# A 4096 x 4096 matmul with gelu: other load order for A, another plan for turning A and for the split operands, and a tail that adds in PSUM

## The chip, the cores and the metric

The kernel runs on one core of a Trainium2 chip. The metric is the device time of one execution in microseconds (us); several executions of each kernel were timed, and medians and ranges are given. Most executions lie within 0.3% of their kernel's median. So differences of a few microseconds out of 1560 need several runs, and the profile's single holes (stretches in which TensorE has no matmul to run) are read beside the times.

TensorE is called PE below, VectorE DVE, ScalarE ACT, GpSimd POOL and SyncE SP. PSUM is the buffer that the matmuls write here. The kernel gives each tile of results (128x512 in f32) a bank of it by name, and the next product writes that bank after another engine has read it out.

## The reference

```python
def setup_inputs():
    m, k, n = 4096, 4096, 4096
    return {"a": np.random.randn(m, k).astype(np.float32),
            "b": np.random.randn(k, n).astype(np.float32)}

def reference(a, b):
    x = np.matmul(a, b)
    return 0.5 * x * (1 + np.tanh(np.sqrt(2 / np.pi) * (x + 0.044715 * x**3)))
```

## The kernel before

The kernel multiplies in f16 with a seven-product scheme. A, B and the output are cut into four quadrants; `A22` is the lower right one. There are 16 **groups**: a block of 512 rows of both row halves of A against a block of 512 columns of both column halves of B. Each group computes M1 to M7, each a product of a sum of two A quadrants with a sum of two B quadrants (or one quadrant alone), from `aS` and `bS`, which DVE makes 2048 elements per partition at a time. In groups 10 to 15 the pair M3/M5, and in groups 13 to 15 also M2/M1, are cut once more by the same scheme; the B operands of that second level ("split operands") are made in earlier groups and parked in DRAM. One **step** of the schedule is 16 matmuls of 512 columns, 3.45 us.

Five parts matter here. *First*, the order in which the first row block is loaded, turned (transposed by DVE) and weighed. `A12_1` is a load of the second K chunk of A12, `T` a transpose, `W` a weighing (ACT squares the rows, to decide at the end whether f16 was safe), `S` a sum:

```python
    for n, whats in (
        (0, "A11_0 B12_0 T11_0 W11_0 B11_0 A21_0 A12_0 B22_0 B21_0"),
        (4, "T21_0 W21_0 A22_0"),
        (6, "T12_0 W12_0"),
        (8, "A11_1+B12_1+B22_1"),
        (9, "T22_0 W22_0 A12_1+B21_1a B21_1b"),
        (14, "T11_1 W11_1 B11_1a A22_1 B11_1b"),
        (16, "T12_1 W12_1:0-4"),
        (17, "W12_1:4-16 A21_1"),
        (18, "S2 S3 T22_1"),
        (23, "T21_1"),
        (34, "W22_1:0-1"),
        # ... one row of W22_1, then of W21_1, a step
```

*Second*, the plan by which later row blocks of A are loaded into one of two staging buffers, turned and weighed; a buffer comes free five steps after its transpose, when ACT has weighed it in four portions:

```python
        free_at = [0, 0]
        for (quad, h), n in zip(halves, turns(gi)):
            at_step(max(n - LOAD_AHEAD, free_at.pop(0)), load, (load_half, (mb, quad, h)))
            free_at.append(n + 5)
            at_step(n, turn_half, mb, quad, h)
            for x in range(4):
                at_step(n + 1 + x, weigh_rows, mb, quad, h, ...)     # cut
            if h and quad in ("12", "21"):
                at_step(n + 5, weigh_half, mb, int(quad[0]) - 1)
```

*Third*, where the split operands are made. An entry of `MAKES` is (group, product, quarter, column block, product it is for); it starts five sums of DVE, one a step, and each goes out to DRAM from one of three `bS` buffers:

```python
MAKES = (
    (6, 1, 0, 1, "M3"), (6, 2, 1, 1, "M5"), (6, 3, 2, 3, "M3"), (6, 4, 2, 3, "M5"),
    (7, 1, 3, 0, "M2"), (8, 2, 3, 2, "M3"), (8, 4, 0, 2, "M5"), (8, 5, 3, 2, "M1"),
    (9, 2, 0, 0, "M3"), (9, 2, 2, 0, "M5"), (9, 4, 2, 3, "M1"), (9, 5, 3, 3, "M2"),
    (10, 2, 2, 2, "M2"), (10, 4, 0, 0, "M1"),
)
```

*Fourth*, `TWO_GROUPS`, the steps at which ACT squares B for the same check. *Fifth*, the end: in the last groups M6 is added on DVE to what M3 and M2 left, and ACT takes the gelu of it:

```python
    def settle_fresh(gi, name, i, X, Y):
        # ... M3, M2, M4 cut
        elif name == "M1":
            m1, x7 = keep("m5", X, 2), post["x7", i]
            tt(x7, x7, m1, ALU.add)
        elif name == "M6":
            y = post.pop(("x1", i))
            tt(y, X, y, ALU.add)
            flush()
            waiting.append((gi, i, 1, 1, y, y))      # gelu and store later
```

## Time and profile before

| | us |
|---|---|
| median of the kernel before, 4 runs | 1572.32 (1568.32 to 1575.03) |
| span of the profiled run | 1570.0 |

The prediction below takes this span apart. I measured holes from start to start: the time between the starts of two matmuls, less the pitch of 215.8 ns (512 columns) or 109.1 ns (256 columns). That counts the half clock too, which the waits do not.

The next lines are PE's instructions in order of time, kernel before: start in us, length, engine, line of the kernel, operation, output <- inputs, shapes, how many; in brackets the idle time before it and what released it.

```profile
85.79 0.61 PE L468 MATMUL accX<-bS,aS 128*128 128x512 f16 x2 [0.55 <-DVE aS L430]
88.40 15.24 PE L468 MATMUL accX<-bS,aS 128*128 128x512 f16 x62 [2.00 <-DVE aS L430]
...
440.58 3.63 PE L468 MATMUL accX<-bR,aS 128*128 128x512 f16 x16 [1.97 <-DVE aS L430]
447.46 26.20 PE L468 MATMUL accX<-bS,aS 128*128 128x512 f16 x120 [1.52 <-ACT m L579]
...
955.48 8.77 PE L468 MATMUL accX<-bK,aS 128*128 128x512 f16 x32 [2.79 <-DVE aS L933]
```

The last row shows how a hole goes on costing: 32 matmuls need 6.9 us at 215.8 ns but took 8.77, because eight of its first eleven ran at half clock. At all of these holes but the one at 447.46 PE waits for DVE, and DVE waits for something else. The list of all waits (engine, what it makes, its line, what released it: us in total, times, longest) names what:

```profile
POOL stage L257 <- ACT stage L271: 106.4, 10, 26.9
...
DVE aT L221 <- DMA stage<-in_a_dram: 69.5, 15, 10.8
...
DVE bS L933 <- DMA k_split<-bS: 26.9, 13, 5.7
```

DVE in order of time shows the same three at the places where PE stood:

```profile
436.45 2.37 DVE L221 STREAM_TRANSPOSE aT<-stage 128x1024 uint32<-128x1024 uint32 x2 [7.23 <-DMA stage<-in_a_dram]
...
942.29 1.23 DVE L933 TENSOR_TENSOR bS<-bK 128x2048 f16<-128x2048 f16 x1 [3.73 <-DMA k_split<-bS]
...
953.06 1.23 DVE L933 TENSOR_TENSOR bS<-bK 128x2048 f16<-128x2048 f16 x1 [2.92 <-DMA k_split<-bS]
```

At 436 the transpose waits for a load that POOL issued late, since its staging buffer was held by ACT's weighing. At 942 and 953 a sum waits until an earlier sum's buffer has been written out.

### The profile page before, as it was taken

To read this page: it belongs to the slowest core of one execution; us is meant where nothing else is said; L and a number is where in the kernel's file an instruction comes from. 1 tells how busy PE (TensorE), PEld (TensorE's weight loads), DVE (VectorE), ACT (ScalarE), POOL (GpSimd) and SP (SyncE) were. 2 spreads that over 40 slices of the span, in tenths; PEclk is the share of its full clock that TensorE was granted. 3 is DMA by queue.
4 is the path that set the end of the run, shared out by engine and by line. 5 is a ranking of instruction groups with operands and counts; after the bars stand their busy time and mean duration, and the time that the engine had idled before them with its cause. 6 is when DMAs were issued, how large, how long until landed. Compare 5 with 4: busy or idle time off the path is not lost. (4 is left out here: it accounts for less than half of the span.)

```text
span 1570.0 us, 22246 instructions
## 1 busy us (share of the span) xinstructions
PE 1547.9 (99%) x8110; PEld 794.1 (51%) x8110; DVE 1139.6 (73%) x1357; ACT 600.8 (38%) x1322; POOL 462.5 (29%) x830
## 2 busy tenths in 40 slices
PE   9999999999999999999999999999999999999998
PEld 4444444444444444444444443554746457677674
DVE  1598888889778886765557647878749677776774
ACT  5446555465643642211554211121355523232232
POOL 7664433431124311122231222221333312132230
PEclk9999999999999999999999999999999999999999
DMA  9999999994789987799998989898999958688692
GB/s 176 183 224 294 269 304 273 286 216 81 188 220 298 292 299 283 278 416 328 277 283 233 411 317 345 307 414 272 279 263 315 351 156 306 237 283 308 234 332 108
DMA packets 202790, 429.41 MB, mean 274 GB/s; under 512 B 20400, under 2 KB 102320, under 8 KB 200624
## 3 DMA queue, kind: packets, MB, share of 16 engines
q0 software_dynamic: 141472, 265.34, 65.6%
q1 hardware_dynamic: 61200, 162.56, 27.1%
q8 instruction: 66, 1.08, 0.3%
q14 instruction: 52, 0.43, 0.1%
HBM read 340.79 MB, written 162.53 MB: 321 GB/s over the span
## 5 line engine op out<-in xcount | busy, mean ns | idle before, releaser
L468 PEld LDWEIGHTS <-aS 128*128 128x128 f16 x4192 | 410.2, 98 | 510.4 <-issue 7.9
L468 PE MATMUL accX<-bK,aS 128*128 128x512 f16 x1536 | 336.0, 380 | 3.3 <-DVE aS L933 3.3
L933 DVE TENSOR_TENSOR aS<-aT 128x2048 f16<-128x2048 f16 x182 | 217.1, 1219 | 94.7 <-PE accX L468 70.6
L468 PEld LDWEIGHTS <-aT 128*128 128x128 f16 x1600 | 156.6, 98 | 189.2 <-issue 1.4
L919 POOL DMA_DIRECT2D bK<-k_M x236 | 124.8, 534 | 401.5 <-PE accX L468 119.3
L257 POOL DMA_DIRECT2D bR<-in_b_dram x320 | 173.1, 543 | 210.5 <-DMA bR<-in_b_dram 98.2
L271 ACT ACTIVATE stage<-stage 128x512 f16<-128x512 f16 (+1 forms) x320 | 169.5, 532 | 141.0 <-DVE aT L221 108.8
L468 PE MATMUL accY<-bK,aS 128*128 128x512 f16 x896 | 195.0, 379 | 2.2 <-DVE aS L933 1.2
L612 ACT ACTIVATE x<-x 128x512 f32<-128x512 f32 x128 | 78.3, 628 | 251.8 <-DVE x L621 251.7
L468 PE MATMUL accX<-bS,aS 128*128 128x512 f16 x704 | 155.1, 382 | 4.1 <-DVE aS L430 2.5
L430 DVE TENSOR_TENSOR aS<-aT 128x2048 f16<-128x2048 f16 (+1 forms) x112 | 134.0, 1201 | 25.8 <-PE accX L468 14.6
L550 PEld LDWEIGHTS <-aS 128*128 128x128 f16 x1440 | 140.9, 98 | 23.1 <-issue 1.1
L430 DVE TENSOR_TENSOR bS<-bR 128x2048 f16<-128x2048 f16 x110 | 133.5, 1218 | 18.6 <-PE accX L468 13.6
L311 ACT ACTIVATE square<-bR 128x1024 bf16<-128x1024 f16 x120 | 123.1, 1048 | 42.7 <-DVE energy L621 42.0
L257 POOL DMA_DIRECT2D stage<-in_a_dram x144 | 84.5, 593 | 178.8 <-ACT stage L271 106.4
L221 DVE STREAM_TRANSPOSE aT<-stage 128x1024 uint32<-128x1024 uint32 (+1 forms) x61 | 76.0, 1278 | 80.0 <-DMA stage<-in_a_dram 69.5
L579 ACT COPY x<-accX 128x512 f32<-128x512 f32 x116 | 67.8, 586 | 173.0 <-PE accX L468 172.7
L933 DVE TENSOR_TENSOR bS<-bK 128x2048 f16<-128x2048 f16 x70 | 84.3, 1219 | 27.1 <-DMA k_split<-bS 26.9
L621 DVE TENSOR_TENSOR x<-accY,x 128x512 f32<-128x512 f32 x116 | 77.2, 688 | 30.1 <-ACT y L612 20.3
L468 PE MATMUL accY<-bK,aT 128*128 128x512 f16 x448 | 97.8, 379 | 0.0
L468 PE MATMUL accX<-bK,aT 128*128 128x512 f16 x448 | 97.8, 379 | 0.0
L579 ACT COPY m<-accX 128x512 f32<-128x512 f32 x76 | 43.2, 581 | 119.8 <-PE accX L468 95.1
(70 smaller groups left out, 1518.4 us busy)
## 6 DMA issues: line engine op xcount, KB each, us to landing
bK<-k_M POOLq DMA_DIRECT2D x272, 512.0 KB, 10.1
bK<-k_split POOLq DMA_DIRECT2D x90, 512.0 KB, 6.7
bR<-in_b_dram POOLq DMA_DIRECT2D x320, 128.0 KB, 7.4
k_M<-bS SPq DMA_DIRECT2D x80, 512.0 KB, 6.5
k_split<-bS SPq DMA_DIRECT2D x70, 512.0 KB, 7.1
out_dram<-y SPq DMA_DIRECT2D x128, 256.0 KB, 6.3
out_dram<-x SPq DMA_DIRECT2D x128, 256.0 KB, 7.3
stage<-in_a_dram POOLq DMA_DIRECT2D x112, 256.0 KB, 8.4
```

The source lines that it names most:

```text
L221: nc.vector.transpose(dst[:, :, x, :], src)
L257: nc.gpsimd.dma_start(out=dst, in_=src)
L271: nc.scalar.activation(src, src, ACT.Square, accum_out=dst)
L311: nc.scalar.activation(t[:, :], src, ACT.Square)
L430: nc.vector.tensor_tensor(out=x, in0=y, in1=z, op=ALU.add if o[2] > 0 else ALU.subtract)
L468: nc.tensor.matmul(acc[:, :], sa[:, j // 2, i * P : (i + 1) * P, j % 2], sb[:, j, :], start=start and j == 0, stop=stop and j == 3, skip_g ...
L550: nc.tensor.matmul(banks[chain, i][:, :] if wide else out, sa[:, j // 2, r * P : (r + 1) * P, j % 2], sb[:, : NC] if wide else sb[:, j * N ...
L579: nc.scalar.copy(out=t[:, :], in_=src[:, :])
L612: nc.scalar.activation(y[:, :], src[:, :], ACT.Gelu_apprx_tanh)
L621: nc.vector.tensor_tensor(out=o[:, :], in0=x[:, :], in1=y[:, :], op=op)
L919: nc.gpsimd.dma_start(out=dst, in_=kept_unit(*key[1:])[:, x * w : (x + 1) * w])
L933: nc.vector.tensor_tensor(out=t, in0=y, in1=z, op=ALU.add if op > 0 else ALU.subtract)
```

## The change

It has five parts: (1) in the first block both halves of A22 are read in runs twice as long and early, before B12 and B22 of the second K chunk, and A12 instead of A22 is weighed late; (2) in the raw groups (those before group 6) A is weighed in two portions, not four, and loaded 8 steps ahead of the transpose, not 7 (9 in the later groups), on another plan of turns, with the squares of B moved; (3) the split operands are placed so that few overlap in a group, with other leads for the sums; (4) B22 is written out for later two products later in group 1; (5) in the last group M3's and M2's part is added by DVE into PSUM before M6's matmuls run on top of it, so that the last gelu reads PSUM directly, and the last tile leaves in two halves on two queues.

```diff
 MAKES = (
-    (6, 1, 0, 1, "M3"),
+    (6, 0, 1, 0, "M3"),
+    (6, 1, 1, 1, "M3"),
     (6, 2, 1, 1, "M5"),
     (6, 3, 2, 3, "M3"),
-    (6, 4, 2, 3, "M5"),
-    (7, 1, 3, 0, "M2"),
+    (7, 0, 1, 2, "M1"),
+    (7, 5, 3, 0, "M2"),
     (8, 2, 3, 2, "M3"),
     (8, 4, 0, 2, "M5"),
-    (8, 5, 3, 2, "M1"),
-    (9, 2, 0, 0, "M3"),
-    (9, 2, 2, 0, "M5"),
-    (9, 4, 2, 3, "M1"),
+    (8, 5, 3, 0, "M5"),
+    (9, 1, 1, 2, "M2"),
+    (9, 2, 2, 3, "M5"),
+    (9, 4, 0, 3, "M1"),
     (9, 5, 3, 3, "M2"),
-    (10, 2, 2, 2, "M2"),
     (10, 4, 0, 0, "M1"),
 )
-SUM_AHEAD = 3
+SUM_AHEAD = 5
-SPLIT_AHEAD = 8
-FETCH_AHEAD = 8
+SPLIT_AHEAD = 6
+FETCH_AHEAD = 9
-LOAD_AHEAD = 7
-TURNS = ((2, 2), (3, 2), (4, 2), (5, 0), (6, 2), (7, 3), (9, 1), (10, 2))
-RAW_TURNS = ((2, 2), (3, 2), (5, 2), (6, 1), (7, 1), (8, 1), (10, 1), (11, 1))
+RAW_LOAD_AHEAD = 8
+WEIGH_STEPS = 2
+LOAD_AHEAD = 9
+TURNS = ((2, 2), (3, 2), (4, 2), (5, 0), (6, 2), (7, 2), (10, 1), (10, 3))
+RAW_TURNS = ((2, 3), (3, 3), (5, 2), (6, 1), (7, 1), (8, 1), (11, 0), (11, 0))
-TWO_GROUPS = [x // 2 for x in range(16)] + [8 + 2 * x for x in range(16)]
+TWO_GROUPS = (0, 0, 1, 1, 2, 2, 3, 3, 4, 4, 4, 4, 5, 5, 5, 5, 5, 7, 10, 12, 14, 16, 18, 18, 20, 20, 24, 26, 27, 27, 28, 29)
+WIDE = "22"
@@ settle_fresh, M1
+            if gi == len(groups) - 1:
+                x1 = post.pop(("x1", i))
+                tt(X, X, x1, ALU.add)
@@ settle_fresh, M6
-        elif name == "M6":
+        elif gi == len(groups) - 1:
+            flush()
+            if i < RT - 1:
+                emit(gi, i, 1, 1, new_y(), X)
+                return
+            # the last tile: r0, c0, w = its row, its column, NC // 2 (cut)
+            for x, queue in enumerate((nc.sync, nc.scalar)):
+                y = new_y()
+                nc.scalar.activation(y[:, :w], X[:, x * w : (x + 1) * w], ACT.Gelu_apprx_tanh)
+                queue.dma_start(out=out[r0 : r0 + P, c0 + x * w : c0 + (x + 1) * w], in_=y[:, :w])
@@ first block
-        (4, "T21_0 W21_0 A22_0"),
+        (4, "T21_0 W21_0 A22_0 A22_1"),
         (6, "T12_0 W12_0"),
-        (8, "A11_1+B12_1+B22_1"),
-        (9, "T22_0 W22_0 A12_1+B21_1a B21_1b"),
-        (14, "T11_1 W11_1 B11_1a A22_1 B11_1b"),
-        (16, "T12_1 W12_1:0-4"),
-        (17, "W12_1:4-16 A21_1"),
-        (18, "S2 S3 T22_1"),
+        (8, "T22_0 W22_0 B12_1+B22_1 A11_1"),
+        (9, "A12_1"),
+        (10, "T22_1 W22_1 B21_1"),
+        (14, "S02 S03 T11_1 W11_1 B11_1"),
+        (16, "T12_1"),
+        (17, "A21_1"),
+        (18, "S22 S23 M22 M23"),
@@ turning of A
-            at_step(max(n - LOAD_AHEAD, free_at.pop(0)), load, (load_half, (mb, quad, h)))
-            free_at.append(n + 5)
+            at_step(max(n - (LOAD_AHEAD if gi >= N_RAW else RAW_LOAD_AHEAD), free_at.pop(0)), load, (load_half, (mb, quad, h)))
+            slow = WEIGH_STEPS if gi < N_RAW else 4
+            free_at.append(n + slow + 1)
@@ keep_raw of M5's B22
-                at(gi, s, 2 * c, keep_raw, nb, name, ob, c)
+                at(gi, s + 2 * (gi == 1 and name == "M5"), 2 * c, keep_raw, nb, name, ob, c)
```

The rest of the diff (how the wide rows are staged, turned and weighed, and the names of the new table) is cut.

More of the change, by code (lines that the diff above doesn't have):

```diff
@@ L214, in turn_a @@
         x = slice(0, NX) if h is None else slice(h * NX // 2, (h + 1) * NX // 2)
-        if mb:
+        if mb or quad == WIDE:
             src = staged[mb, quad, h].rearrange("p x (c r) -> p c x r", c=CH)[:, c]
@@ L292, in weigh_first @@
             k = ((kh * CH + c) * 2 + ih) * NX + x
+            if quad == WIDE:
+                k = (kh * CH * 2 + ih) * NX + c * NX // 2 + x
             weigh_row(stats["a"][:, k : k + 1], staged[0, quad, c][:, x, :])
@@ L682, in settle_fresh @@
             waiting.append((gi, i, 0, 0, y, y))
-        elif name == "M6":
+        elif gi == len(groups) - 1:
[3 more added lines that the diff above has]
+                return
+            mb, nb = groups[gi]
+            r0, c0, w = MH + mb * TM + i * P, NH + nb * NC, NC // 2
+            for x, queue in enumerate((nc.sync, nc.scalar)):
+                y = new_y()
+                nc.scalar.activation(y[:, :w], X[:, x * w : (x + 1) * w], ACT.Gelu_apprx_tanh)
+                queue.dma_start(out=out[r0 : r0 + P, c0 + x * w : c0 + (x + 1) * w], in_=y[:, :w])
+        else:
             y = post.pop(("x1", i))
@@ L723, in half_path @@
         (0, "A11_0 B12_0 T11_0 W11_0 B11_0 A21_0 A12_0 B22_0 B21_0"),
-        (4, "T21_0 W21_0 A22_0"),
+        (4, "T21_0 W21_0 A22_0 A22_1"),
         (6, "T12_0 W12_0"),
-        (8, "A11_1+B12_1+B22_1"),
-        (9, "T22_0 W22_0 A12_1+B21_1a B21_1b"),
-        (14, "T11_1 W11_1 B11_1a A22_1 B11_1b"),
-        (16, "T12_1 W12_1:0-4"),
-        (17, "W12_1:4-16 A21_1"),
-        (18, "S2 S3 T22_1"),
-        (23, "T21_1"),
-        (34, "W22_1:0-1"),
-        (35, "W22_1:1-2"),
-        (36, "W22_1:2-3"),
-        (37, "W22_1:3-4"),
-        (38, "W22_1:4-5"),
-        (39, "W22_1:5-6"),
-        (40, "W22_1:6-7"),
-        (41, "W22_1:7-8"),
-        (42, "W22_1:8-9"),
-        (43, "W22_1:9-10"),
-        (44, "W22_1:10-11"),
-        (45, "W22_1:11-12"),
-        (46, "W22_1:12-13"),
-        (47, "W22_1:13-14"),
-        (48, "W22_1:14-15"),
-        (49, "W22_1:15-16"),
+        (8, "T22_0 W22_0 B12_1+B22_1 A11_1"),
[5 more added lines that the diff above has]
+        (18, "S22 S23 M22 M23"),
+        (23, "T21_1"),
+        (34, "W12_1:0-1"),
+        (35, "W12_1:1-2"),
+        (36, "W12_1:2-3"),
+        (37, "W12_1:3-4"),
+        (38, "W12_1:4-5"),
+        (39, "W12_1:5-6"),
+        (40, "W12_1:6-7"),
+        (41, "W12_1:7-8"),
+        (42, "W12_1:8-9"),
+        (43, "W12_1:9-10"),
+        (44, "W12_1:10-11"),
+        (45, "W12_1:11-12"),
+        (46, "W12_1:12-13"),
+        (47, "W12_1:13-14"),
+        (48, "W12_1:14-15"),
+        (49, "W12_1:15-16"),
         (50, "W21_1:0-1"),
@@ L766, in half_path @@
         for what in whats.split():
-            half = what[-1] == "0" and what != "A11_0" or what in ("A22_1", "T22_1")
-            if what[0] == "S":
-                before.setdefault(n, []).append((make_sums, (0, 2, int(what[1]), "bS")))
+            if what[0] in "SM":
+                args = (0, int(what[1]), int(what[2]), {"S": "bS", "M": "aS"}[what[0]])
+                before.setdefault(n, []).append((make_sums, args))
                 continue
+            wide = what[1:3] == WIDE and what[0] != "B"
             if what[0] == "W":
-                xs = range(*(int(x) for x in what[6:].split("-"))) if what[6:] else range(NX)
+                rows = range(NX // 2) if wide else range(NX)
+                xs = range(*(int(x) for x in what[6:].split("-"))) if what[6:] else rows
                 before.setdefault(n, []).append((weigh_first, (what[1:3], int(what[4]), xs)))
                 continue
+            if wide:
+                args = (0, WIDE, int(what[4]))
+                if what[0] == "T":
+                    before.setdefault(n, []).append((turn_half, args))
+                else:
+                    before.setdefault(n, []).append((load, [(load_half, args)]))
+                continue
+            half = what[-1] == "0" and what != "A11_0"
             for h in (0, 1) if half else (None,):
@@ L781, in half_path @@
                     before.setdefault(n, []).append((turn_a, args[0][1]))
-                    if what == "T22_1":
-                        for q in range(QPH // 2, QPH):
-                            before[n].append((make_sums, (0, 2, q, "aS", h)))
                 else:
@@ L828, in half_path @@
         for (quad, h), n in zip(halves, turns(gi)):
-            at_step(max(n - LOAD_AHEAD, free_at.pop(0)), load, (load_half, (mb, quad, h)))
-            free_at.append(n + 5)
+            at_step(max(n - (LOAD_AHEAD if gi >= N_RAW else RAW_LOAD_AHEAD), free_at.pop(0)), load, (load_half, (mb, quad, h)))
+            slow = WEIGH_STEPS if gi < N_RAW else 4
+            free_at.append(n + slow + 1)
             at_step(n, turn_half, mb, quad, h)
-            for x in range(4):
-                at_step(n + 1 + x, weigh_rows, mb, quad, h, list(range(NX // 2))[x * NX // 2 // 4 : (x + 1) * NX // 2 // 4])
+            for x in range(slow):
+                at_step(n + 1 + x, weigh_rows, mb, quad, h, range(x * NX // 2 // slow, (x + 1) * NX // 2 // slow))
             if h and quad in ("12", "21"):
-                at_step(n + 5, weigh_half, mb, int(quad[0]) - 1)
+                at_step(n + slow + 1, weigh_half, mb, int(quad[0]) - 1)
     for nb, gi in last_raw.items():
@@ L1156, in half_path @@
         warm()
+        nc.vector.memset(stats["a"][:, :], 0.0)
         table = pool.tile([P, 1], F32, name="table", tag="table")
```

## The prediction

> **What bounds the kernel now.** I read the engine table and the slices of the page first, then PE's own waits, then PE's order in time, and last the granted clock in single stretches. Page, part 1 and the clock row:
>
> ```profile
> PE 1547.9 (99%) x8110; PEld 794.1 (51%) x8110; DVE 1139.6 (73%) x1357; ACT 600.8 (38%) x1322; POOL 462.5 (29%) x830
> ...
> PEclk9999999999999999999999999999999999999999
> ```
>
> PE has work 99% of the time, at nearly full clock, and no other engine exceeds 73%. So the time is PE's matmul stream plus its holes. What the stream costs without holes is read from a chain row of three undisturbed products: 13.81 us for 64 matmuls of 512 columns is 215.8 ns each, and 3.49 us for 32 of 256 columns is 109.1 ns each. The order of instructions has, on the path that runs, 6084 matmuls of 512 columns and 1980 of 256 after the 46 warm-ups: 6084 x 0.2158 + 1980 x 0.1091 = 1529 us. The first starts at 14.08 us, so a stream without holes ends at about 1543 us; it ends at 1563.3 us. That leaves **20 us of holes**, and 6.7 us of tail up to the end of the span at 1570.0. PE's waits:
>
> ```profile
> PE accX L468 <- DVE aS L430: 5.0, 4, 2.0
> PE accX L468 <- DVE aS L933: 3.3, 2, 2.8
> PE accX L468 <- ACT m L579: 1.5, 1, 1.5
> ...
> PE accY L468 <- DVE aS L933: 1.2, 1, 1.2
> PE accX L550 <- DVE x L621: 0.9, 1, 0.9
> ```
>
> They sum to 14.0 us after the warm-up. They are not spread: PE's order in time puts 3.9 us in block group 0 (35 to 88 us), 3.7 us in group 4 (440 to 485), 1.2 at 751, 4.3 in group 9 (949 to 993) and 0.9 at 1201; no PE wait follows. The other 6 us are not in this list. Some are the ends of matmuls, which the profile models about 0.17 us late, so that each of the 13 waits is shorter in it than the gap from start to start. The rest is clock, in the stretches table (stretch, its length, PE busy, clock, DMA):
>
> ```profile
> 88.40:92.40 4.00, 4.00 (x11) 0.57 1.42 192
> 92.60:100.00 7.40, 7.40 (x36) 1.00 1.24 202
> 440.60:444.60 4.00, 4.00 (x19) 1.00 0.27 105
> ...
> 955.50:959.40 3.90, 3.90 (x11) 0.56 1.03 420
> ```
>
> After the longest holes (2.0 us at 88.40, with 0.55 just before, and 2.79 at 955.48) the clock is 0.57 and 0.56 for 4 us and the matmuls go 427 ns apart: 8 or 9 x 0.21 = 1.9 us lost each time, though PE is "busy". After the 1.97 us at 440.58 it stays 1.00. In start-to-start gaps the holes are: group 0 6.7, group 4 4.4, group 7 1.4, group 9 6.7, group 11 1.0; sum 20.2 us.
>
> [...]the trace shows half clock after holes of 2.2 (with another just before) and 2.9 us[...] the row of aS has 1219 ns[...] the loads of f32 into f16 here write 200 GB/s, that is, read 400 GB/s, in the first 100 us[...].
>
> **The change part by part.** PE's rows are the same in both programs, in order and size (18278), so the 1529 us stay. DVE has 1495 instructions instead of 1496, ACT 14 fewer. Only holes and the tail can move.
>
> *First block.* Both halves of A22 are now read in 2 KB runs, the second already before B12 and B22 of the second K chunk, and A11 and A12 of that chunk come after B, not between. The old hole came from the second chunk of A22 landing last, at 84 us, with M7 waiting for its transposes and sums. That chunk is early now, so M7's 2.0 + 0.55 us and the half clock after them (together 4.9 us) go. But M3 now needs 12.6 MB landed instead of 11.6 (f16, counted in queue order). In the old trace 12.6 MB have landed at 71.5 us; a transpose of 2.31 us then gives 73.8, and M3 starts at 70.0: a new hole of 3.8 us, and half clock again, 5.7 together. Against that, the loads dipped to some 148 GB/s from 56 to 65 us while GpSimd waited between interleaved issues; without this dip 9 x (1 - 148/195) = 2.2 us come back, and long runs (packets of 1024 B took 98 ns, of 512 B 60 ns, by throughput 200 against 190 GB/s) save 0.6: then the hole is 1.0 us. I take two in three for the second: 0.65 x 1.0 + 0.35 x 5.7 = 2.7, plus the 0.6 at 35.41, whose loads are unchanged. Group 0: 6.7 to 3.3.
>
> *Turning A.* In group 4 DVE stood 7.2 us at the transpose of A22, which GpSimd had issued late because its staging buffer was weighed by ACT over four steps (a stage load waited 26.6 us for ACT there). Two steps and the longer lead issue that load 5 steps of 3.45 us ahead instead of 3, 17 us against a landing of some 8; the energy sums leave this group too. 4.4 to 0.4.
>
> *Split operands.* In group 9 two makes of five sums overlapped (steps 8-12 and 10-14), each sum written out by a DMA that lands in 7.1 us, from 3 buffers: DVE waited for them 3.7, 0.9, 2.9 and 2.5 us, PE behind it. Now no two of that group share a step: one per 3.45 us and 3 buffers give 10.3 us per reuse, over 7.1. Group 9 6.7 to 0.4. Group 7's 1.4 was the same wait and its makes move away: 0.
>
> *Group 11.* DVE was busy without a break from 1176.6 to 1201. Before the evacuation that PE waits for it has two sums fewer, 2.3 us against 1.0 of hole: 1.0 to 0.3.
>
> *Tail.* The last output loses DVE's 0.69 us and half of a 0.63 us activation, but gains a second half activation beside it: about 0.7 us less. The four added additions in PSUM lie under the 13.8 us of M4.
>
> Sum: -3.4 -4.0 -1.4 -6.3 -0.7 -0.7 = -16.5; new small holes from a plan that moves hundreds of sums: +1. So **1573.3 - 15.5, about 1558 us**.
>
> **Rivals.** (a) *The hole only moves to M3*, with the half clock: group 0 would keep 6.3 and the time be about 1561. For it: more bytes before M3. (b) *DVE becomes the limit at another place*, for instance where both halves of A21 are turned in one step of group 4 (4.7 us of transposes in a 3.45 us step beside 5.3 us of combinations), or where sums are made only 6 steps ahead: 2 to 5 us back, about 1561. Against: DVE waits 2.7 us for a DMA just there. (c) *It brings nothing*: the waits are behind DMA landings that come anyway. Against: [...]the waits were for buffers, not for bandwidth.
>
> **Range and chances.** All holes gone would be 1573.3 - 20.2 - 0.7 = 1552.4, so 1553 is the low end. Rivals (a) and (b) together and a median at the upper end of the spread (1571.4 to 1575.0) make 1565. Over 2% would be 31 us, more than all holes and the tail allow; 2% slower would need holes to be more than doubled.
>
> **What would show it.** Right: PE's list of waits under 5 us in all, none at 440, 949 or 955, a clock of 1.00 there, and the last gelu reading accX. Wrong: a wait for aT or aS at 70 to 74 us with a clock near 0.57 after it; the k_split wait of DVE still above 2 us in group 9; a new wait at about 475 to 485 us; or a granted clock that is lower throughout, which no part of this argument covers.

## The result

| kernel | median us | range | runs |
|---|---|---|---|
| before | 1572.32 | 1568.32 to 1575.03 | 4 |
| changed | 1556.74 | 1553.62 to 1558.60 | 4 |

The ratio is 0.9901 with a 95% interval of 0.9873 to 0.9929: 1% faster. A ratio here is the mean time of one kernel's fast runs over that of the other's of the same rounds, so it is not quite the ratio of the two medians.

The engine table of the changed kernel, to hold against that of before:

```profile
PE 1541.9 (99%) x8110; PEld 793.2 (51%) x8110; DVE 1139.6 (73%) x1356; ACT 598.0 (39%) x1291; POOL 453.8 (29%) x814
```

The number of PE instructions and DVE's busy time are unchanged. PE's busy time is 6.0 us less for the same matmuls. Of this 3.4 us are the half clock after the holes (16 matmuls at 427 instead of 216 ns) and about 1.5 us the modelled ends of matmuls ahead of nine holes more, about 0.17 us each. The other 1.0 us is the warm-up, 46 matmuls on zeros before the data are there: in the kernel before 13 of them ran at half clock, in the changed one 9, and in before_again, the kernel before unchanged, 7, so the number varies without an edit (see the end of the part on why the prediction was right). All waits of PE in the changed kernel:

```profile
PE accY L504 <- DVE aT L224: 1.7, 2, 1.5
PE accX L485 <- DVE zeros L480: 1.4, 1, 1.4
PE accY L473 <- DVE x L626: 1.3, 1, 1.3
PE accY L504 <- DMA bR<-in_b_dram: 0.6, 1, 0.6
```

Without the start of the warm-up (zeros) that is 3.6 us, and all of it lies in the first block; PE's instructions in order of time:

```profile
48.84 3.63 PE L504 MATMUL accY<-bR,aT 128*128 128x512 f16 x16 [0.24 <-DVE aT L224]
53.96 17.44 PE L504 MATMUL accY<-bR,aT 128*128 128x512 f16 x80 [1.49 <-DVE aT L224]
72.69 7.07 PE L473 MATMUL accY<-bS,aT 128*128 128x512 f16 x32 [1.28 <-DVE x L626]
```

The hole at 88 us is gone and three others stand before it. DVE's order shows why M3 waits at 72.69: the transpose of A11's second chunk, which had to wait 4.1 us for its load, comes ahead of four additions that free M3's banks.

```profile
69.75 2.31 DVE L224 STREAM_TRANSPOSE aT<-stage 128x2048 uint32<-128x2048 uint32 x1 [4.11 <-DMA stage<-in_a_dram]
71.99 2.44 DVE L626 TENSOR_TENSOR x<-x,accY 128x512 f32<-128x512 f32 x4
```

In group 9 one wait for a buffer of a split operand is left, the row that answers to 3.73 and 2.92 us of before:

```profile
938.57 1.23 DVE L961 TENSOR_TENSOR bS<-bK 128x2048 f16<-128x2048 f16 x1 [1.13 <-DMA k_split<-bS]
```

The end of the program, first before, then changed (ACTq is ACT issuing a transfer):

```profile
1564.09 0.63 ACT L612 ACTIVATE x<-x 128x512 f32<-128x512 f32 x1 [0.23 <-DVE x L621]
```

```profile
1546.96 0.66 ACT L700 ACTIVATE y<-accX 128x256 f32<-128x256 f32 x2 [0.27 <-PEq L1217]
...
1547.65 0.38 ACTq L701 DMA_DIRECT2D out_dram<-y  x1
```

The last gelu now follows PE, not an addition of DVE.

The holes of these two profiles, from start to start, by group (us; the tail is the time from the end of the last matmul to the end of the span; my working from the traces; the stretches that are not listed add 0.13 us):

| | first matmul at | group 0 (to 131 us) | group 4 | group 7 | group 9 | after 1000 us | sum | tail |
|---|---|---|---|---|---|---|---|---|
| before | 14.08 | 6.54 | 4.39 | 1.38 | 6.57 | 1.18 | 20.2 | 6.65 |
| changed | 13.19 | 4.28 | 0.02 | 0.02 | 0.05 | 0.13 | 4.6 | 5.14 |

The spans differ by 18.0 us: 15.6 of holes, 1.5 of tail, 0.9 of an earlier first matmul. The medians differ by 15.6, so these two profiles overstate it a little: the profiled run of the changed kernel was the fastest of its four. Which of these terms belong to the change, and to which part, is what the experiments ask.

### The profile page after: what moved, and what is told of

Read it like the earlier page. It is cut to its first block, busy times and chain, and to the rows that moved or that the text cites.

```text
span 1552.0 us, 22240 instructions
## 1 busy us (share of the span) xinstructions
PE 1541.9 (99%) x8110; PEld 793.2 (51%) x8110; DVE 1139.6 (73%) x1356; ACT 598.0 (39%) x1291; POOL 453.8 (29%) x814
## 5 line engine op out<-in xcount | busy, mean ns | idle before, releaser
L961 DVE TENSOR_TENSOR aS<-aT 128x2048 f16<-128x2048 f16 x182 | 217.4, 1219 | 92.5 <-PE accX L473 60.6
L947 POOL DMA_DIRECT2D bK<-k_M x228 | 120.6, 533 | 411.1 <-PE accX L473 114.9
L435 DVE TENSOR_TENSOR aS<-aT 128x2048 f16<-128x2048 f16 x110 | 133.8, 1219 | 31.7 <-PE accX L473 20.5
L260 POOL DMA_DIRECT2D stage<-in_a_dram x136 | 79.9, 595 | 144.6 <-ACT stage L274 111.1
L961 DVE TENSOR_TENSOR bS<-bK 128x2048 f16<-128x2048 f16 x70 | 84.3, 1217 | 27.5 <-DMA k_split<-bS 27.3
```

The source lines that it names most:

```text
L260: nc.gpsimd.dma_start(out=dst, in_=src)
L435: nc.vector.tensor_tensor(out=x, in0=y, in1=z, op=ALU.add if o[2] > 0 else ALU.subtract)
L947: nc.gpsimd.dma_start(out=dst, in_=kept_unit(*key[1:])[:, x * w : (x + 1) * w])
L961: nc.vector.tensor_tensor(out=t, in0=y, in1=z, op=ALU.add if op > 0 else ALU.subtract)
```

## The experiments

Twelve runs were made, in three calls, each call on one chip beside the kernel before. All outputs were correct. The table gives the holes of every profile in the same way, but for the two runs with holes made on purpose; the arguments below rest on it. The wait before the first matmul is in its start and not in group 0.

| run | span | group 0 | group 4 | group 7 | group 9 | after 1000 us | tail |
|---|---|---|---|---|---|---|---|
| undo_first_block | 1554.1 | 3.56 | 0.02 | 0.02 | 0.05 | 1.00 | 5.41 |
| undo_turning | 1563.7 | 6.48 | 3.94 | 0.01 | 0.05 | 4.97 | 5.18 |
| undo_split | 1562.7 | 5.32 | 0.03 | 0.23 | 5.10 | 3.14 | 5.91 |
| undo_tail | 1554.0 | 4.39 | 0.02 | 0.02 | 0.05 | 0.79 | 5.89 |
| only_raw | 1560.3 | 2.24 | 0.02 | 0.57 | 7.54 | 0.64 | 6.09 |
| only_squares | 1562.5 | 3.82 | 2.83 | 0.52 | 6.17 | 0.14 | 5.99 |
| only_makes | 1556.6 | 3.16 | 2.68 | 0.02 | 0.05 | 1.94 | 6.08 |
| before_again | 1572.7 | 4.23 | 4.06 | 1.11 | 5.68 | 7.74 | 6.72 |
| after_again | 1554.5 | 4.15 | 0.02 | 0.01 | 0.05 | 1.58 | 5.56 |
| better | 1557.3 | 3.63 | 0.03 | 0.02 | 0.05 | 5.69 | 5.43 |

### First call: one part of the change undone

The kernel before had a median of 1569.56 us here (7 runs, 1564.60 to 1582.70), so the intervals are wide. The changed kernel itself, 1556.74 us, comes from another chip; undo_tail, 1557.06 us, is the nearest mark.

| run | median us | range | runs | ratio to before | 95% interval |
|---|---|---|---|---|---|
| undo_first_block | 1557.09 | 1555.61 to 1560.35 | 4 | 0.9911 | 0.9841 to 0.9980 |
| undo_turning | 1560.60 | 1559.46 to 1565.38 | 4 | 0.9924 | 0.9856 to 0.9993 |
| undo_split | 1564.51 | 1562.38 to 1566.21 | 4 | 0.9951 | 0.9881 to 1.0020 |
| undo_tail | 1557.06 | 1554.84 to 1560.09 | 4 | 0.9909 | 0.9839 to 0.9979 |

**undo_first_block.** The changed kernel with the load order of before in the first block:

```diff
-WIDE = "22"
-        (4, "T21_0 W21_0 A22_0 A22_1"),
+        (4, "T21_0 W21_0 A22_0"),
-        (8, "T22_0 W22_0 B12_1+B22_1 A11_1"),
-        (9, "A12_1"),
-        (10, "T22_1 W22_1 B21_1"),
+        (8, "A11_1+B12_1+B22_1"),
+        (9, "T22_0 W22_0 A12_1+B21_1a B21_1b"),
         # ... and so on, the whole table of before
```

> The changed kernel with the first block as before (A22 of it in short runs, the old order of loads and turns, the old places of its weighing); everything else as changed. If the parts are separate, only the holes of PE before 131 us come back: gaps of 6.7 us in all (0.6 at 35, then 72, 78, 86, 88) with a clock near 0.57 after 88 us, instead of 4.2 us without half clock: about 2.4 us longer. Rival: the gain in the first block came from the other constants (squares earlier, SUM_AHEAD), then the gaps stay near 4 us.

It took 1557.09 us against 1556.74 for the changed kernel: no difference that can be seen. With four runs that spread over 5 us the times alone would not show 2 to 3 us; the holes of all profiles decide it at the end. Its holes are back at M7, but without the half clock that was expected:

```profile
87.00 1.47 PE L470 MATMUL accX<-bS,aS 128*128 128x512 f16 x6 [1.72 <-DVE aS L432]
88.88 12.25 PE L470 MATMUL accX<-bS,aS 128*128 128x512 f16 x56 [0.40 <-ACT m L581]
```

So the first block's holes are 3.56 us with the old order and 4.28 with the new. The rival named above, that the other constants had brought them down, is not needed: the kernel before, profiled again with none of them changed, has 4.23. The prediction had reckoned with a dip of the loads between 56 and 65 us, which the new order would fill. The stretch from 56 to 66 us in the table of stretches (stretch, its length, busy time and instructions of PE, PEld, DVE, ACT and POOL, clock, DMA share, GB/s), first in the kernel before, then here:

```profile
56.00:66.00 10.00, 10.00 (x48) 4.52 (x47) 0.72 (x2) 0.00 (x0) 6.93 (x12) 1.00 1.11 149
```

```profile
56.00:66.00 10.00, 10.00 (x48) 4.54 (x47) 2.51 (x3) 0.00 (x0) 8.20 (x15) 1.00 1.30 193
```

With the same load order the dip is not there. The other four profiles with the old order have 180 to 199 GB/s in this stretch, the seven with the new order 172 to 194 (without the variant `better`). The dip belonged to that one profile, not to the order.

**undo_turning.** The changed kernel with four portions of weighing, the leads, the raw turns and the squares of before:

```diff
-RAW_LOAD_AHEAD = 8
-WEIGH_STEPS = 2
-LOAD_AHEAD = 9
+LOAD_AHEAD = 7
-RAW_TURNS = ((2, 3), (3, 3), (5, 2), (6, 1), (7, 1), (8, 1), (11, 0), (11, 0))
+RAW_TURNS = ((2, 2), (3, 2), (5, 2), (6, 1), (7, 1), (8, 1), (10, 1), (11, 1))
-TWO_GROUPS = (0, 0, 1, 1, ...)
+TWO_GROUPS = [x // 2 for x in range(16)] + [8 + 2 * x for x in range(16)]
```

> The changed kernel with the old plan of turning A in groups 3 and 4 (four weighing steps, lead of 7 steps, old turn steps) and the old places of the squares of B. Theory: the gaps at 440, 447 and 484 us come back, 4.4 us in all, nothing elsewhere. Rival: other parts of the change relieve DVE there as well, then less than 2 us come back.

```profile
73.94 8.75 PE L471 MATMUL accY<-bS,aT 128*128 128x512 f16 x32 [2.50 <-DVE x L624]
...
440.19 3.63 PE L471 MATMUL accX<-bR,aS 128*128 128x512 f16 x16 [1.80 <-DVE aS L433]
```

Group 4 has its 3.94 us of holes again, and the median is 3.9 us up (3.5 above undo_tail). The profiled run was the slowest of the four (1565.38), since in it M3's hole was 2.50 us instead of 1.28 and halved the clock (32 matmuls in 8.75 us instead of 7.07), and 5 us were lost after 1000 us. The edit does not touch the first block, and the other three runs of the same kernel are 4 to 6 us faster, so most of this varies from run to run. What the shorter lead in the later groups (7 instead of 9) adds after 1000 us can't be told from one profile.

**undo_split.** The changed kernel with `MAKES`, the leads of the sums and the later turns of before:

```diff
-    (9, 1, 1, 2, "M2"),
-    (9, 2, 2, 3, "M5"),
-    (9, 4, 0, 3, "M1"),
+    (9, 2, 0, 0, "M3"),
+    (9, 2, 2, 0, "M5"),
+    (9, 4, 2, 3, "M1"),
     # ... and the other entries, SUM_AHEAD = 3, SPLIT_AHEAD = 8, FETCH_AHEAD = 8, TURNS
```

> The changed kernel with the old list of split operands (two made in the same steps of group 9), the old lead constants and the old turn steps of the later groups. Theory: the gaps of groups 7, 9 and 11 come back, 1.4 + 6.7 + 1.0 = 9 us, with a clock near 0.57 for 4 us after the longest; by far the largest part. Rival: the gaps depend on where DVE stands after the earlier holes, which are gone; then much less than 9 us returns.

PE's and DVE's rows in group 9:

```profile
947.47 8.77 PE L473 MATMUL accX<-bK,aS 128*128 128x512 f16 x32 [2.29 <-DVE aS L961]
```

```profile
934.95 1.23 DVE L961 TENSOR_TENSOR bS<-bK 128x2048 f16<-128x2048 f16 x1 [3.40 <-DMA k_split<-bS]
```

The wait of DVE for its buffer, PE's hole and the half clock after it (8.77 us again) are back, 5.10 us in all, and the median is 7.8 us up (7.5 above undo_tail). This is the largest single part. Of the 9 us expected, groups 7 and 9 gave 5.3: group 7 came back with only 0.23, so for group 7 this run shows little. Another 3.14 us were lost after 1000 us, where other kernels lose as much without this edit (see `better`).

**undo_tail.** The changed kernel with M1 and M6 of the last group as before:

```diff
-            if gi == len(groups) - 1:
-                x1 = post.pop(("x1", i))
-                tt(X, X, x1, ALU.add)
-        elif gi == len(groups) - 1:
-            # ... gelu straight from X
-        else:
+        elif name == "M6":
```

> The changed kernel with the last outputs as before (addition by DVE, then one gelu of 512 columns, one queue). Predicted 0.7 us longer from the last matmul to the end; the profile of the changed kernel against the one before suggests 1.5 us. Holes of PE unchanged at about 4.6 us. Rival: the last DMA and what follows it set the tail, then no difference.

The time is the same to 0.3 us, too little to tell. The tail of the profile is: six profiles with the old end have 5.89 to 6.72 us, mean 6.24; six with the new end have 5.14 to 5.91, mean 5.44. So the new end saves 0.8 us on average, about as much as a tail varies by itself.

### Second call: one part alone on the kernel before, and holes made on purpose

Each ran once beside one run of the kernel before (1564.12 us, which is low for it: the call before this one has 1564.60 to 1582.70). The state of a single run is unknown, so these are judged by their traces alone: only_raw 1561.92 us, only_squares 1564.08, only_makes 1558.18.

**only_raw** tests whether the weighing and the leads alone remove group 4's holes:

```diff
-LOAD_AHEAD = 7
+RAW_LOAD_AHEAD = 8
+WEIGH_STEPS = 2
+LOAD_AHEAD = 9
-RAW_TURNS = ((2, 2), (3, 2), (5, 2), (6, 1), (7, 1), (8, 1), (10, 1), (11, 1))
+RAW_TURNS = ((2, 3), (3, 3), (5, 2), (6, 1), (7, 1), (8, 1), (11, 0), (11, 0))
```

> The kernel before with only the staging part of the turning plan (two weighing steps, lead of 8 steps, new turn steps); squares of B stay where they were. Theory (staging buffers came free late): the gaps at 440 and 447 us, 3.9 us in start-to-start, go, with the wait of DVE for the stage load of 7.2 us; the one at 484 may stay or grow to 1 us, since two halves are now turned in one step. Rival (DVE was overloaded by the sums of squares): over half of the 3.9 us stays.

They do, together with the new turn steps: 0.02 us of holes in group 4, and no wait of PE between 400 and 500 us. The transpose that stood at 436.45 comes 9.7 us earlier; DVE still waits there, but early enough. Group 9, which this leaves alone, has its hole:

```profile
426.71 2.37 DVE L223 STREAM_TRANSPOSE aT<-stage 128x1024 uint32<-128x1024 uint32 x2 [5.85 <-DMA stage<-in_a_dram]
```

```profile
946.62 9.84 PE L470 MATMUL accX<-bK,aS 128*128 128x512 f16 x32 [3.34 <-DVE aS L936]
```

**only_squares** tests the rival, that the squares and their sums on ACT and DVE were what held group 4 up:

```diff
-TWO_GROUPS = [x // 2 for x in range(16)] + [8 + 2 * x for x in range(16)]
+TWO_GROUPS = (0, 0, 1, 1, 2, 2, ...)
```

> The kernel before with only the squares of B moved to other steps. Theory: the gaps at 440 and 447 us stay within 1 us of 3.9. Rival (DVE overloaded by the sums of squares): over half goes.

```profile
436.76 3.63 PE L468 MATMUL accX<-bR,aS 128*128 128x512 f16 x16 [1.09 <-DVE aS L430]
443.03 26.20 PE L468 MATMUL accX<-bS,aS 128*128 128x512 f16 x120 [0.92 <-ACT m L579]
```

2.83 us stay in group 4, just outside the 1 us around 3.9 that was expected, and DVE waits 8.47 us for the staged A there. The rival is refuted as the cause, since less than half went. Whether it helps a little is not settled: only_makes, which leaves the squares as they were, has 2.68 there, against 4.39 and 4.06 in the two profiles of the kernel before.

**only_makes** tests whether the overlap of two makes alone caused groups 7 and 9, without the other leads:

```diff
 MAKES = (   # the list of the changed kernel; SUM_AHEAD, SPLIT_AHEAD, FETCH_AHEAD and TURNS as before
```

> The kernel before with only the list of split operands changed, so that two are not made in the same steps of group 9; leads and turn steps as before. Theory (three buffers and a 7 us write each were overbooked): the gaps of groups 7 and 9 go, 8.1 us, the 1.0 us at 1201 stays. Rival (the longer lead of sums is needed as well): over 3 us of the 8.1 stay.

Groups 7 and 9 have 0.02 and 0.05 us. So the list of makes is enough; the other leads are not needed for it. Group 9 has four makes in both lists, so it is not their number: in the old list two of them share three steps, in the new one none do. Where the waits for buffers went is told by DVE's waits in stretches: in the kernel before, DVE waits 5.7 us for `k_split` between 680 and 800 us and 16.8 between 800 and 1000; in the changed kernel 12.4 and 7.4. The longest in the changed kernel is this one:

```profile
714.58 1.22 DVE L961 TENSOR_TENSOR bS<-bK 128x2048 f16<-128x2048 f16 x1 [6.82 <-DMA k_split<-bS]
```

Over the whole program these waits are 26.9 us before and 27.3 us after. The total did not fall. The waits moved to steps where DVE has nothing due behind them that PE waits for: PE has no hole there.

**holes** asks what decides whether a hole also halves the clock, because the prediction read a threshold from two cases. In 20 steps of groups 5 to 9 of the changed kernel a small chain of DVE operations was put between PE's last result and its next operand:

```diff
+    def hole(step, tens):
+        h = pool.tile([P, 128], F32, name="hole", tag="hole")
+        nc.vector.memset(h[:, :], 0.0)
+        nc.vector.tensor_copy(out=h[:, :1], in_=banks[chain, RT - 1][:, :1])   # waits for PE
+        for _ in range(tens // 3):
+            nc.vector.tensor_tensor(out=h[:, :], in0=h[:, :], in1=h[:, :], op=ALU.max)
+        nc.vector.tensor_copy(out=sa[:, :2], in_=sa[:, :2])                    # PE waits for this
```

> The changed kernel with twenty holes put into PE's stream on purpose, in groups 5 to 9, some 28 us apart: DVE takes a bank of the step before, spends 0 to 3.3 us (nominal), and only then gives the next operand free. Result stays right. Theory: holes over about 2.1 us are followed by 4 us at a clock near 0.57 (8 to 9 matmuls at 427 ns, 1.9 us more), shorter ones are not, so a hole of 2.5 us costs 4.4. [...]Rival 2: it is a matter of chance[...], then holes of equal length differ.

48 matmuls after a hole take 10.54 us at full clock and 12.22 if the clock was halved at first:

```profile
738.08 12.22 PE L473 MATMUL accY<-bK,aS 128*128 128x512 f16 x48 [4.02 <-DVE aS L1199]
...
807.33 10.54 PE L473 MATMUL accY<-bK,aS 128*128 128x512 f16 x48 [2.06 <-DVE aS L1199]
...
976.13 10.54 PE L473 MATMUL accY<-bK,aS 128*128 128x512 f16 x48 [3.91 <-DVE aS L1199]
```

A hole of 3.91 us leaves the clock alone and one of 4.02 does not; of two at 3.85 us from start to start both halved it. The holes came out longer than planned (queued sums of 1.2 us stood between), so few short ones were among them, and a second series was needed. The time, 1678.44 us, says only that 20 holes cost a lot.

### Third call: both kernels again, a variant, and short holes

**before_again** and **after_again** are the two kernels unchanged, to see how much a profile varies by itself.

> The kernel before, unchanged, profiled once more. In four profiles of kernels with its first block the gaps before 131 us were 4.5, 2.2, 3.8 and 3.2 us, in its own first profile 6.5. If that first profile was an unlucky one, this one shows under 5 us there and 4 to 8 us in group 9, about 4 in group 4. If it was typical, over 6 us before 131 us and half clock after 88 us.

> The changed kernel, unchanged, timed in five rounds as the mark for the next one, and profiled once more: gaps of 4 to 6.5 us before 131 us, none from 400 to 1000 us, 0.1 to 1 us at about 1186 us, tail of 5.1 to 5.5 us. Time 0.989 to 0.992 of before.

What was expected of the two came, but for two small things in after_again: a loss of 1.58 us after 1000 us (0.1 to 1 expected) and a tail of 5.56 us (5.1 to 5.5 expected). after_again had a median of 1556.16 us (5 runs, 1554.45 to 1558.90), ratio 0.9907 with an interval of 0.9887 to 0.9927 to the kernel before, which had 1571.67 (11 runs, 1567.59 to 1574.42). That repeats the result with a narrower interval. Groups 4, 7 and 9 repeat within 0.9 us in the kernel before (4.06, 1.11, 5.68) and are empty again in the changed one. Two terms do not repeat. Group 0 of the kernel before is 4.23 instead of 6.54, since the hole of 1.55 us at M7 did not halve the clock. And after 1000 us the kernel before loses 7.74 us instead of 1.18, at the boundary of groups 10 to 12:

```profile
1179.46 14.06 PE L468 MATMUL accY<-bK,aS 128*128 128x512 f16 x64 [2.49 <-DVE aS L933]
...
1202.01 5.54 PE L550 MATMUL accX<-bK,aS 128*128 128x512 f16 x32 [3.03 <-DVE x L621]
```

The changed kernel loses 1.58 there in its second profile, 0.13 in its first. In each of these profiles DVE stands 8.5 to 13.2 us twice at the transposes for the next row block, then works almost without a break up to this boundary. DVE's wait for the staged A between 1000 and 1250 us is the same in both first profiles, kernel before and then changed:

```profile
DVE aT L221 <- DMA stage<-in_a_dram: 22.2, 4, 9.8
```

```profile
DVE aT L224 <- DMA stage<-in_a_dram: 22.5, 3, 9.4
```

So the change left this stretch on the edge where it was: `WEIGH_STEPS = 2` applies to the raw groups alone, and here ACT still weighs in four portions.

**better** tries to close the hole at M3 (two transposes cut in two, so that DVE can free M3's banks between) and moves one of group 11's transposes:

```diff
-TURNS = ((2, 2), (3, 2), (4, 2), (5, 0), (6, 2), (7, 2), (10, 1), (10, 3))
+TURNS = ((2, 2), (3, 2), (4, 2), (5, 0), (7, 1), (7, 2), (10, 1), (10, 3))
-        (14, "S02 S03 T11_1 W11_1 B11_1"),
-        (16, "T12_1"),
-        (17, "A21_1"),
+        (14, "S02 S03 T11_1:0-0 B11_1"),
+        (15, "T11_1:0-2"),
+        (16, "T11_1:2-4 W11_1 T12_1:0-0 T12_1:0-2"),
+        (17, "T12_1:2-4 A21_1"),
```

> The changed kernel with two things mended: the transposes of A11 and A12 of the second chunk in two halves, each in front of the quarter that reads it and behind the evacuations that PE waits for; and one transpose of A22 in groups 7 and 11 moved three steps later, behind the evacuations that PE waits for at about 1190 us. Theory (DVE's order is what PE waits for): the gap at 73 us falls from 1.0 to 2.5 us to under 0.5, that at 1186 to 1195 us to under 0.3; 1.5 to 2.5 us less in time. Rival (the data land too late anyway): the gap at 73 us stays over 1 us.

The median is 1556.75 us (6 runs, 1553.49 to 1560.62), ratio 0.9907: no better than the changed kernel, so of the three things expected only the first came. The hole at 73 us is gone from the list of waits, which shows that DVE's order was its cause. But group 0 still has 3.63 us, of which 1.56 is A22's transpose, and the boundary, where the other transpose was moved, has 5.69 us in this profile against 0.13 and 1.58 in the changed kernel:

```profile
1186.93 3.87 PE L559 MATMUL accX<-bK,aS 128*128 128x512 f16 x32 [1.52 <-DVE x L630]
...
1201.54 3.65 PE L559 MATMUL accY<-bK,aS 128*128 128x256 f16 x32 [2.02 <-DVE accY L573]
```

Whether the moved transpose did that, or the stretch's own spread, one profile does not tell. All twelve profiles together speak for the spread. DVE's two long waits for the staged A come ahead of the boundary. Together they were 16.0 to 18.9 us in the three profiles that lose least after 1000 us (0.13 to 0.64), 19.5 to 21.4 in the six that lose 0.79 to 3.14, and 22.9 to 24.6 in the three that lose most (4.97, 5.69 for better, 7.74). The first wait in the changed kernel, then in better:

```profile
1141.69 2.37 DVE L224 STREAM_TRANSPOSE aT<-stage 128x1024 uint32<-128x1024 uint32 x2 [9.44 <-DMA stage<-in_a_dram]
```

```profile
1145.24 2.37 DVE L228 STREAM_TRANSPOSE aT<-stage 128x1024 uint32<-128x1024 uint32 x2 [13.51 <-DMA stage<-in_a_dram]
```

The load behind it goes out in four parts, from 1128.7 to 1130.4 us in the one and from 1128.2 to 1131.3 in the other, but the last part lands at 1141.6 and at 1145.1. So a load that lands late comes before the loss. No run changed the landing time alone, so this is a relation over twelve profiles and not a test. What the first half gained is not in the time, and the changed kernel stands.

**holes_short** repeats the deliberate holes in groups 1 to 5, shorter:

```diff
-    LENGTHS = [0, 12, 24, 6, 18, 30, 9, 21, 15, 27, 3, 33, 18, 24, 21, 15, 27, 12, 30, 18]
+    LENGTHS = [2, 9, 5, 7, 3, 10, 6, 8, 4, 11, 7, 9, 5, 8, 6, 10, 3, 7, 9, 8]
-        for _ in range(tens // 3):
+        for _ in range(tens):
         # and the call stands at the start of the step, ahead of DVE's other work in it
```

> Twenty holes again, shorter, in groups 1 to 5, placed ahead of the other work of DVE in that step. With the first series (none of 1.9, 2.2, 2.9, 3.5 and 4.1 us tripped the clock; 3.85 us did twice and all of 4.2 and more) the theory is now [...]holes under about 2 us never trip it, over 4.2 us always, and between the two some do and some don't, more of the longer ones. Rival: a fixed threshold near 3.8 us, then nothing below it trips.

```profile
529.56 12.22 PE L473 MATMUL accX<-bS,aS 128*128 128x512 f16 x48 [2.29 <-DVE aS L1199]
```

Here a hole of 2.29 us was enough (2.46 from start to start). The time, 1655.49 us in one run, says no more than that of holes. Over the 40 holes of both kernels, measured from start to start:

| hole, us | holes | followed by half clock |
|---|---|---|
| 1.15 to 2.13 | 7 | 0 |
| 2.23 to 4.07 | 14 | 10 |
| 4.12 to 6.81 | 19 | 19 |

In the middle range both 2.45 (halved) and 4.07 (one halved not, two halved) occur. No fixed threshold, neither about 2.1 nor about 3.8 us, puts these in order. The half clock costs mostly 1.4 to 1.7 us after the hole (7 or 8 matmuls at 427 ns), at most 2.9 (14 matmuls). That is what was expected of this series: none of the 7 up to 2.13 us halved the clock, all 19 from 4.12 us on did, and of the 14 between 3 of the 5 under 3 us and 7 of the 9 over it. Why holes of equal length differ there was not shown; what the hardware counts stays open.

## Why the prediction was right, and where it was wrong

The time was right: about 1558 us predicted, from 1573.3 as the median of the three runs known then, and 1556.74 measured; 15.5 us of gain predicted and 15.6 measured. One of its steps was wrong and one is not settled, so that the numbers agree so closely is partly luck.

- **A fixed stream of 1529 us.** Right. In the stretches without holes the excess is 0.06 us in 240 us, in every profile.
- **"Group 0: 6.7 to 3.3."** This is the step that failed. The first profiles seem to give 2.3 of the 3.4 us, but undoing it costs nothing that shows (1557.09 against 1556.74 us). Over the six profiles with the old order group 0 has 2.24 to 6.54 us, mean 3.9; over the five of the tables with the new order (without the variant) 4.15 to 6.48, mean 4.9. These means leave no room for a gain of 3.4. It failed in three ways. The base of 6.7 held a half clock, taken as 1.9 us (8 matmuls, 1.7 by the trace), that only one of the six profiles has; the dip of the loads that the step let the change fill was in that one profile; and while the hole did move to M3, as rival (a) said (1.0 to 2.7 us from start to start in the five, against 1.0 or 3.8 taken; better shows that DVE's order made it, not bytes alone), a second one at A22's transpose (0.24 + 1.49 us, much the same in all five) was not foreseen.
- **Turning A, "4.4 to 0.4".** Right: 0.02 or 0.03 us in every kernel that has it, 2.7 to 4.4 in every one that has not. only_raw shows that the weighing, the leads and the turn steps together do it, not the squares; which of the three is enough was not tried.
- **Split operands, "Group 9 6.7 to 0.4", group 7 to 0.** Right: 0.05 and 0.02 us. For group 9 this is shown both by undoing and by doing only the list. For group 7 it rests on only_makes: kernels with the old list have 0.23 to 1.38 us there. The test named for it, no wait for `k_split` above 2 us in group 9, holds with 1.13.
- **Group 11, "1.0 to 0.3".** Not settled. The kernel before loses 1.18 or 7.74 us after 1000 us and the changed one 0.13 or 1.58, and in the four kernels with a part undone it is 0.79 to 4.97. The spread of one kernel there is larger than the 0.7 us in question. The term taken, two sums fewer ahead of the boundary, leaves out how late the loads ahead of it land, which goes with the loss (see `better`).
- **Tail, 0.7 us.** Right: 0.8 on average. That M6's matmuls keep what DVE has added in PSUM was the author's assumption in the prediction. The runs of the changed kernel show it for this order: in the last group DVE adds four times into accX (0.69 us each, 1519.21 to 1523.51 us), M6's 64 matmuls accumulate on that from 1532.90 us on, and the outputs were correct in all runs.
- **"New small holes: +1."** None came: outside the listed stretches the excess stays at 0.13 us in all. In this pair of profiles that 1 us, the 0.9 us of an earlier first matmul and a tail 0.8 us better than predicted stand against what the first block did not give. In the medians the account does not close: groups 4, 7 and 9 (mean of two profiles of the kernel before) and the tail are 12.3 of the 15.6 us. The rest is not shown; the stretch after 1000 us, where the kernel before lost 1.18 and 7.74 and the changed one 0.13 and 1.58, is the largest candidate in the profiles.

Rival (b), DVE as the limit elsewhere, was not seen at 475 to 485 us, where it was to show. Rival (c) is refuted by groups 4 and 9.

That the first matmul starts anywhere between 13.2 and 14.8 us is no part of the change. It starts when the 46 warm-up matmuls are done and its data are there. Of the warm-up 7 (before_again) to 13 (the first profile of before) matmuls ran at half clock, so that it ended between 12.9 and 14.2 us; where the data came later still, PE waited for their load (1.02 us in before_again).

What stays open: whether weighing in two portions in the later groups too would bring the stretch at 1180 to 1202 us off its edge, and why the loads ahead of it land up to 3.6 us later in one run than in another.

## What to carry to other kernels

When the bound engine is busy 99% of the time and its instructions can't change, list its holes one by one, follow each back to the buffer that was late, and put work elsewhere in the schedule: the same 27 us of waits cost 8 us in one order and nothing in another. Before a hole's size goes into a sum, look at it in a second profile of the same kernel: here the holes that a plan caused repeated within 1 us, and those on an edge varied by 2 to 7. A part of a change that looks good in one pair of profiles is shown only when it is undone, and, where the times spread more than its gain, when its holes are compared over several profiles.
